# A hybrid retention, attention and expert layer on one core: the modulation products as four strips of 32 columns, a fifth row buffer, norm scaling on ScalarE, and a new order

## The chip, the core and the metric

The kernel runs on one core of one Trainium2 chip. A core has a matrix engine (TensorE, PE in the profile; its weight loads are listed apart as PEld), VectorE (DVE), ScalarE (ACT), GpSimd (POOL) and SyncE (SP), which work at the same time and wait for one another through semaphores. Operands lie in an on-chip memory of 128 partitions (SBUF); PE adds its results up in banks of a second one (PSUM). The transfers from and to the large memory (HBM) are done by 16 DMA engines; here SP issues most of them, and POOL those that gather rows by index. The metric is the device time of one execution in microseconds (us), the median of several runs.

## What is computed

One layer for 1024 latent tokens and 256 context tokens of width D = 1024, in fp32. Cut to what matters:

```python
mod   = silu(c)     @ w_mod + b_mod        # 6 x 1024 numbers: shift, scale, gate, twice
mod_c = silu(c_ctx) @ w_mod + b_mod        # for the context tokens: shift and scale are used
h  = rms_norm(x,   norm1_g) * (1 + mod[1])   + mod[0]
hc = rms_norm(ctx, norm1_g) * (1 + mod_c[1]) + mod_c[0]
rq, rk, rv, rg, dq, dk, dv = split(h @ w_in)       # the same for hc
y  = concat(retention_both_ways(...), differential_attention(...))
x  = x + mod[2] * (y @ w_out)
h2 = rms_norm(x, norm2_g) * (1 + mod[4]) + mod[3]
q  = h2 @ w_query                          # 8 heads, two halves of 128
experts, gate = top 16 of the sums of the top 16 by two sets of 128 keys
x  = x + mod[5] * sum_j gate_j * gelu(peer_u[experts_j] . h2) * peer_v[experts_j]
```

`w_mod` has 1024 x 6144 numbers (24 MB). There are 128 x 128 = 16384 experts, each a row of 1024 numbers in `peer_u` and in `peer_v`, and each token uses 8 x 16 = 128 of them.

## The kernel before

**How the order of the work comes about.** The kernel does not issue its instructions as it reads. A recording layer (class `Plan`, lines 162 to 590) keeps each operation as a node, with a cost in us by a table of rules (`cost`, line 281), and a list scheduler (`schedule`, line 332, run several times) places them on the five engines by rank. Ranks come from the order of recording; where several stages are to overlap, `weave` (line 207) merges their recordings, each stretched over a span of the others from a pair of constants (`QSPAN`, `ASPAN`, `GSPAN`, `G2SPAN`, `HSPAN` and others at the top of the file). Then all is issued in the planned order from one line (590; 591 in the changed kernel), so every instruction of the trace shows that line and groups are told apart by the names of their tiles. SBUF tiles come from pools by tag, each with a number of buffers (`bufs`, line 602); a tile waits until one of its tag is free.

**Stages.** The 10 blocks of 128 tokens are 8 latent ones (0 to 7) and 2 of the context.

1. *The start.* Five blocks are loaded and scaled by their norms (`norm_rows`, line 675: two squares with sums on ScalarE, the power -0.5 on GpSimd, the scaling on VectorE). The first 2048 columns of `w_mod` come in 8 chunks of 1024 x 256 (1 MB, two `wst` tiles each, which has 4 buffers, `wstream`, line 666). For each chunk, 8 products add up in one PSUM tile: the weights are `sc[:, k, :]`, 128 rows of which only 2 columns are used (silu of `c` and of `c_ctx`), the moving operand is 128 x 256 of `w_mod`. The two rows go to `mrow`, 16 transposes turn them to columns (`modT`), and `token_cols` (715) applies them.
2. *Projections.* `project3` (860) multiplies five key blocks by chunks of `w_in`, then the five others: each fp32 factor is split into two fp32r parts (ACT takes the high part, DVE the rest), and three products stand for one (`three`, 851). That split recurs in the dense phase.
3. *Retention* (1005), with the queries of block 0 (`late_queries`, 960) and `spread(0)` to `spread(2)` (1068) woven in. A spread does four more chunks of `w_mod` as above, for one of the four vectors `mod[2..5]`, adds the bias and stores the row in HBM; `spread(3)` is woven into the routing of block 0.
4. *By groups of blocks* (0; 4 and 5; 6 and 7; 3; 1 and 2): `attend`, `mix` (output projection), `route` (queries and key scores), `select` (1283: the top 16, by many small DVE steps), and, for blocks 3 to 7, `gates` (1417), which lays the gates out as a dense table `Wd` in HBM.
5. *The dense phase* (1500) for blocks 3 to 7: all 16384 experts by products, in 32 groups of 4 x 128 experts; each group loads 4 rows of `peer_u`, 4 of `peer_v` (all split) and its part of `Wd`.
6. *Gathered rows* for blocks 0, 1 and 2 (`halves`, 1368), beside stages 4 and 5: 2 x 3 x 128 = 768 times POOL gathers 128 rows of `peer_u` or `peer_v` by index into a tile of 128 x 1024 (512 KB), and DVE does one step on it: a product with a sum along the row (`gat,act<-gat,h2t`), or the sum `acc<-gat,act,acc`. The tiles are taken from the tag `gat` (4 buffers) or, when more than 5 of its 8 are free, from `h`. In a window of the plan (`HOLD`) POOL issues no gathers, so that the selection and the gates have DVE.

Of the kernel before, what the change touches and what calls it, by code (L numbers as in the profile page):

```python
# [31 lines left out]
HOLD = [1000, 1550]  # L32
# [20 lines left out]
QSPAN = [[-0.2, 0.475], [0.1, 1], [-0.1, 1.309], [-0.35, 1.05], [0.15, 0.9]]  # L53
ASPAN = [[0.05, 1.424], [0.05, 1.05], [0.15, 1], [0, 1.104]]
GSPAN = [[0.3, 1], [-0.15, 0.754], [0.15, 1.248], [-0.1, 1.2], [-0.3, 0.02]]
DSPAN = [0.02, 0.0, 0.05]
LSPAN = [[0.479, 1.05], [0.565, 1.218], [0.436, 1.3], [0.05, 0.85]]
G2SPAN = [0.182, 0.991]
VL, CL, EC, XE = 'D', 'D', 'D', 'PPPPPPPP'
POFF, PACES = 40, [[0, 3.6], [200, 2.25], [300, 1.17], [700, 1.18], [1100, 1.9]]  # L60
# [8 lines left out]
HSPAN = [[-0.25, 1.0], [0.05, 0.796], [0.2, 1.588]]  # L69
# [92 lines left out]
class Plan:  # L162
# [118 lines left out]
    def cost(self, eng, meth, a, k, outs, vs):  # L281
# [19 lines left out]
        if eng == "PE":  # L301
# [6 lines left out]
            return 4 * max(n, 64) * (0.5 if n >= 256 and a[1].shape[0] == 64 else 1) / 2330.0, 0, None, False  # L308
# [288 lines left out]
def layer(tc, I, out, dbg=None):  # L597
# [3 lines left out]
    with sp as S, pp as P, dp as DR:  # L601
        bufs = {"mm": 8, "h": 8, "k": 5, "rv": 4, "b": 4, "v": 5, "sel": 3, "wst": 4, "gat": 4, "fin": 2,  "u1": 3, "u2": 2, "u3": 2,
                "o": 1, "vi": 2, "egb": 3, "pt": 2, "m4": 4, "s1": 2, "act": 2,  "gsum": 2, "rs": 2, "ssum": 2, "ff": 3}
# [15 lines left out]
        def ps(shape):  # L619
            return nc.tile(shape, F32, "mm")  # L620
# [36 lines left out]
        cc = sb([128, KD, 2], "cc")  # L657
# [5 lines left out]
        sc = sb([128, KD, 2], "sc")  # L663
        nc.scalar.activation(sc, cc, AF.Silu)
# [10 lines left out]
        def norm_rows(kb, tag):  # L675
# [11 lines left out]
            nc.vector.tensor_scalar(xt, xt, ms[:, 2:3], None, op0=OP.mult)  # L687
# [5 lines left out]
        rcol = sb([128, 24], "rcol")  # L693
# [3 lines left out]
        mrow = [sb([2, D], "rv") for _ in range(2)]  # L697
        for ch in range(8):
            w = wstream(wm, ch * 256)
            pm = ps([2, 256])  # L700
            with nc.unit():
                for k in range(KD):
                    nc.tensor.matmul(pm, sc[:, k, :], w[k], start=(k == 0), stop=(k == KD - 1))
            nc.scalar.copy(mrow[ch // 4][:, ch % 4 * 256:(ch % 4 + 1) * 256], pm)
        mt = ps([128, 16, 2])
        with nc.unit():
            for n in range(16):
                nc.tensor.transpose(mt[:, n, :], mrow[n // 8][:, n % 8 * 128:(n % 8 + 1) * 128], ident[0:2, 0:2])
# [44 lines left out]
        dist = sb([128, 2, 128], "vi")  # L753
        nc.sync.dma_start(dist, I["k_dist"])
# [6 lines left out]
        retg = sb([128, 512], "pt")  # L761
        nc.sync.dma_start(retg, row_bcast(I["ret_norm_g"], 512))
# [869 lines left out]
```

## Time and profile before

| what | us |
|---|---|
| median of 3 runs (lowest to highest) | 3445.88 (3432.36 to 3452.61) |
| the profiled execution's own time | 3449.74 |
| its span in the trace | 3447.9 |
| ACT busy, of the span | 1330.9 (39%) |
| POOL busy, of the span | 1115.0 (32%) |
| the costliest group: `mm<-k,h` on PE, 4096 records (the dense phase's products with `peer_u`) | 925.5 |
| transfers | 809.69 MB, 235 GB/s in the mean |

The mean granted clock of TensorE was 0.960 of full speed. In rows of groups, `out<-in` are tile names (buffer numbers left out): `mm` is any PSUM tile, `wst` a buffer of streamed weights, `sc` the two condition vectors, `rv` and `h` are shared by many uses (in the start `rv` holds the two modulation rows, in the dense phase `h` holds split expert rows), `gat` the gathered rows, `egb` the expert indices. `x384 | 86.1, 379` are the count, the busy us and the mean ns of one; what follows is the idle time just before them and what ended it. An fp32 product shows as two records.

### The profile page before, as it was taken

Reading aid. Unit: us, or ns where it says so; the run is one execution under the profiler, and the core shown is the slowest. Engines: PE = TensorE matmul, PEld = TensorE weight load, DVE = VectorE, ACT = ScalarE, POOL = GpSimd, SP = SyncE. Lnnn points to the kernel's source line nnn. Section 1 sums busy time; section 2 is a strip of 40 time slices with the busy share of each in tenths; the row PEclk is TensorE's granted clock in tenths of the full one; section 3 lists DMA queues with packets and bytes.
Section 4 is the critical chain, followed back from the end, with each engine's and each line's share of the span. In section 5 each row is a group of like instructions: output and inputs, shape, how many; then the busy total and the mean of one; then the engine's idle time right before and its main releaser. Section 6 shows DMA issues by size and latency. Waiting matters only on the chain. (4 is left out here: it accounts for less than half of the span.)

```text
span 3447.9 us, 51507 instructions
## 1 busy us (share of the span) xinstructions
PE 3151.3 (91%) x18240; PEld 2732.3 (79%) x18240; DVE 2654.8 (77%) x5963; ACT 1330.9 (39%) x3535; POOL 1115.0 (32%) x1099
## 2 busy tenths in 40 slices
PE   7999997779789888897899999999999999999998
PEld 4998575557677766887788888989898889788887
DVE  4457546879997978666978888788888887878797
ACT  4342443425269898753212222222222222222221
POOL 0101111443440201103544444344444443444341
PEclk9999998889999998999999999999999999999999
DMA  5322655777584642654888889798888887878886
GB/s 184 97 82 88 214 194 169 262 272 238 182 292 155 217 138 93 219 194 159 287 296 275 308 273 307 244 305 282 298 287 310 278 307 271 283 258 296 284 289 207
DMA packets 314532, 809.69 MB, mean 235 GB/s; under 512 B 29313, under 2 KB 125593, under 8 KB 314274
## 3 DMA queue, kind: packets, MB, share of 16 engines
q1 hardware_dynamic: 203682, 403.70, 35.1%
q0 software_dynamic: 110592, 402.70, 34.3%
q8 instruction: 144, 2.36, 0.3%
q14 instruction: 114, 0.93, 0.1%
HBM read 745.46 MB, written 60.83 MB: 234 GB/s over the span
## 5 line engine op out<-in xcount | busy, mean ns | idle before, releaser
L590 PE MATMUL mm<-k,h 128*128 128x384 f32 (+1 forms) x4096 | 925.5, 311 | 34.4 <-DVE h L590 32.1
L590 PEld LDWEIGHTS mm<-k,h 128*128 128x128 f32 x4096 | 700.0, 189 | 46.9 <-DVE h L590 33.8
L590 POOL DMA_INDIRECT gat<-peer_v,egb x379 | 465.2, 1227 | 640.8 <-DVE acc L590 432.2
L590 ACT CAST h<-wst 128x512 fp32r<-128x512 f32 (+1 forms) x384 | 286.6, 762 | 895.4 <-PE mm L590 869.3
L590 PE MATMUL mm<-v,h 128*128 128x384 f32 (+1 forms) x2048 | 632.1, 309 | 0.0
L590 POOL DMA_INDIRECT gat<-peer_u,egb x369 | 439.0, 1190 | 589.4 <-DVE gat L590 386.1
L590 PE MATMUL mm<-h,rv 128*128 128x512 f32 x2304 | 602.1, 399 | 17.5 <-DVE rv L590 12.4
L590 DVE SCALAR_TENSOR_TENSOR acc<-gat,act,acc 128x1024 f32<-128x1024 f32 x376 | 483.2, 1285 | 64.1 <-DMA gat<-peer_v,egb 62.6
L590 PEld LDWEIGHTS mm<-h,rv 128*128 128x128 f32 x2304 | 425.1, 190 | 119.4 <-DVE rv L590 21.4
L590 DVE SCALAR_TENSOR_TENSOR gat<-gat,h2t 128x1024 f32<-128x1024 f32 x369 | 452.3, 1231 | 48.2 <-DMA gat<-peer_u,egb 47.8
L590 DVE TENSOR_TENSOR h<-wst,h 128x512 fp32r<-128x512 f32 (+1 forms) x384 | 329.3, 867 | 204.9 <-issue 109.4
L590 PE MATMUL mm<-h,t 128*128 128x512 f32 (+1 forms) x1600 | 419.8, 393 | 26.8 <-DVE b L590 16.9
L590 PEld LDWEIGHTS mm<-v,h 128*128 128x128 f32 x2048 | 387.5, 189 | 7.9
L590 PEld LDWEIGHTS mm<-h,t 128*128 128x128 f32 x1600 | 294.4, 189 | 100.3 <-DVE b L590 22.7
L590 POOL TENSOR_TENSOR m<-m,mhalf 128x4 f32<-128x4 f32 (+1 forms) x78 | 75.5, 970 | 771.2 <-DVE m L590 761.5
L590 PE MATMUL mm<-b,wst 128*128 128x256 f32 (+1 forms) x1280 | 237.3, 340 | 0.6 <-ACT h L590 0.3
L590 PEld LDWEIGHTS mm<-b,wst 128*128 128x128 f32 x1280 | 204.0, 192 | 24.3 <-ACT u L590 2.6
L590 ACT CAST rv<-aT 128x384 fp32r<-128x384 f32 x128 | 65.8, 514 | 355.8 <-DVE aT L590 349.8
L590 DVE TENSOR_TENSOR b<-b,mm 128x512 f32<-128x512 f32 x248 | 164.9, 682 | 43.8 <-PE mm L590 43.6
L590 PE MATMUL mm<-t,h 128*128 128x256 f32 x992 | 186.8, 287 | 6.7 <-DVE aT L590 3.5
L590 PEld LDWEIGHTS mm<-t,h 128*128 128x128 f32 x992 | 158.1, 193 | 8.0 <-DVE aT L590 3.7
L590 PE MATMUL mm<-wst,h 128*128 128x256 f32 x560 | 156.5, 297 | 0.0
(239 smaller groups left out, 4714.5 us busy)
## 6 DMA issues: line engine op xcount, KB each, us to landing
wst<-peer_u_cols SPq DMA_DIRECT2D x128, 512.0 KB, 7.1
wst<-peer_v_halves SPq DMA_DIRECT2D x128, 512.0 KB, 4.5
wst<-w_query_chunks SPq DMA_DIRECT2D x80, 512.0 KB, 5.3
h<-Wd SPq DMA_DIRECT2D x64, 512.0 KB, 9.7
wst<-w_mod_chunks SPq DMA_DIRECT2D x48, 512.0 KB, 5.2
wst<-w_out_chunks SPq DMA_DIRECT2D x40, 512.0 KB, 7.1
Wd<-rv SPq DMA_DIRECT2D x40, 512.0 KB, 6.8
Wd<-gat SPq DMA_DIRECT2D x40, 512.0 KB, 5.7
```

The source lines that it names most:

```text
L590: getattr(handles[n.eng], meth)(*[res(v) for v in a], **k)
```

## The change

It has four parts. The computation stays the same.

1. **Strips.** `sc` becomes 128 x 8 x 32 with zeros in all but two columns of each 32 (in the tag `ob`, set to zero by DVE). A new function `conditioned` does the 8 products of a chunk: product k goes to partitions 32 (k mod 4) and on of one PSUM tile, so that four sums of two products each lie in four strips of 32 partitions. All 128 partitions are copied. A selector `pick` (128 x 2, ones in rows 32 g and 32 g + 1, made from the identity) adds the four strips: in the start 16 products with 128 x 128 weights and `pick` as the moving operand take the place of the 16 transposes of 2 x 128; in a spread two products with one column of `pick` as weights and 512 moving columns are new, and the bias is added from PSUM in two steps of 1 x 512. The planner's cost of such a product is set to 0.3 of a full one.
2. **A fifth `gat` buffer** (2 MB to 2.5 MB for the tag). Small tiles move to tags that exist: `cc`, `rcol`, `t8`, `sc`, one of two tiles in `gates`, and the retention's mask and gain (`t4`, `t6`), which are now computed and loaded at the beginning of `retention` and not in the start.
3. **Norm scaling** in `norm_rows` moves from DVE to ACT (18 calls).
4. **Order.** `HOLD` ends at 1500 of the plan and not 1550; some pairs of the spans change. (`QSPAN[4]` is not used, and the last entry of `PACES` begins at step 1100 of 768.)

```diff
-HOLD = [1000, 1550]
+HOLD = [1000, 1500]
-HSPAN = [[-0.25, 1.0], [0.05, 0.796], [0.2, 1.588]]
+HSPAN = [[-0.4, 1.0], [0.05, 1.096], [0.2, 1.888]]
...
-            return 4 * max(n, 64) * (0.5 if n >= 256 and a[1].shape[0] == 64 else 1) / 2330.0, 0, None, False
+            side = 0.3 if outs[0].shape[0] == 32 else 0.5 if n >= 256 and a[1].shape[0] == 64 else 1
+            return 4 * max(n, 64) * side / 2330.0, 0, None, False
...
-        bufs = {"mm": 8, "h": 8, "k": 5, "rv": 4, "b": 4, "v": 5, "sel": 3, "wst": 4, "gat": 4, "fin": 2,  "u1": 3, "u2": 2, "u3": 2,
+        bufs = {"mm": 8, "h": 8, "k": 5, "rv": 4, "b": 4, "v": 5, "sel": 3, "wst": 4, "gat": 5, "fin": 2,  "u1": 3, "u2": 2, "u3": 2,
...
-        sc = sb([128, KD, 2], "sc")
-        nc.scalar.activation(sc, cc, AF.Silu)
+        sc = sb([128, KD, 32], "ob")
+        nc.vector.memset(sc, 0.0)
+        nc.scalar.activation(sc[:, :, 0:2], cc, AF.Silu)
+        pick = sb([128, 2], "pick")
+        nc.vector.tensor_reduce(out=pick, in_=ident.rearrange("p (g c) -> p c g", c=32)[:, 0:2, :], axis=AX.X, op=OP.add)
+        def conditioned(w):
+            pm = ps([128, 256])
+            with nc.unit():
+                for k in range(KD):
+                    g = k % 4 * 32
+                    nc.tensor.matmul(pm[g:g + 32, :], sc[:, k, :], w[k], start=(k < 4), stop=(k >= 4))
+            return pm
...
-            nc.vector.tensor_scalar(xt, xt, ms[:, 2:3], None, op0=OP.mult)
+            nc.scalar.activation(xt, xt, AF.Copy, scale=ms[:, 2:3])
...
-        mrow = [sb([2, D], "rv") for _ in range(2)]
+        mrow = [sb([128, D], "rv") for _ in range(2)]
         for ch in range(8):
             w = wstream(wm, ch * 256)
-            pm = ps([2, 256])
-            with nc.unit():
-                for k in range(KD):
-                    nc.tensor.matmul(pm, sc[:, k, :], w[k], start=(k == 0), stop=(k == KD - 1))
-            nc.scalar.copy(mrow[ch // 4][:, ch % 4 * 256:(ch % 4 + 1) * 256], pm)
+            nc.scalar.copy(mrow[ch // 4][:, ch % 4 * 256:(ch % 4 + 1) * 256], conditioned(w))
...
-                nc.tensor.transpose(mt[:, n, :], mrow[n // 8][:, n % 8 * 128:(n % 8 + 1) * 128], ident[0:2, 0:2])
+                nc.tensor.matmul(mt[:, n, :], mrow[n // 8][:, n % 8 * 128:(n % 8 + 1) * 128], pick, start=True, stop=True)
...
-                nc.scalar.copy(row[:, ch * 256:(ch + 1) * 256], pm)
-            nc.vector.tensor_tensor(out=row[0:1, :], in0=row[0:1, :], in1=bro, op=OP.add)
+                nc.scalar.copy(row[:, ch * 256:(ch + 1) * 256], conditioned(w))
+            for half in range(2):
+                hs = slice(half * 512, (half + 1) * 512)
+                pm = ps([1, 512])
+                nc.tensor.matmul(pm, pick[:, 0:1], row[:, hs], start=True, stop=True)
+                nc.vector.tensor_tensor(out=bro[:, hs], in0=bro[:, hs], in1=pm, op=OP.add)
...
-                    o1 = sb([128, 4, 128], "t4" if q % 2 else "o")
+                    o1 = sb([128, 4, 128], "t4" if q % 2 else "t7")
```

Three places show how the order moves. The first is PE's queue from the program's beginning in the kernel before (`mm<-wst,sc` are the chunk products, `mm<-ident,rv` the transposes of the two rows, `mm<-ident,k` those of token blocks):

```order
L590 MATMUL mm<-ident,k 128x128
L590 MATMUL mm<-ident,act 128x24
L590 MATMUL mm<-ident,k 128x128 x15
L590 MATMUL mm<-wst,sc 2x256 x64
L590 MATMUL mm<-ident,rv 128x2 x16
L590 MATMUL mm<-ident,k 128x128 x24
```

And in the changed kernel, where `sc` lies in a tile of the tag `ob`:

```order
L591 MATMUL mm<-ident,act 128x24
L591 MATMUL mm<-ident,k 128x128 x8
L591 MATMUL mm<-wst,ob 32x256 x16
L591 MATMUL mm<-ident,k 128x128 x8
L591 MATMUL mm<-wst,ob 32x256 x48
L591 MATMUL mm<-pick,rv 128x2 x16
L591 MATMUL mm<-ident,k 128x128 x24
```

The first two chunks now stand between the transposes of token blocks, and the products with `pick` where the transposes of the rows stood. The second place is DVE's queue in the second dense group, before (`h<-wst,h 128x1024` is a split of one row of `peer_u`; `sel` belongs to the selection of block 2). The split at the end of these rows is that of the row numbered 7; the last split ahead of it stands 67 instructions earlier, and 17 of the 66 between are steps on gathered rows:

```order
L590 TENSOR_TENSOR sel<-sel 128x800
L590 SCALAR_TENSOR_TENSOR acc<-gat,act,acc 128x1024
L590 TENSOR_REDUCE sel<-sel 128x4x4
L590 SCALAR_TENSOR_TENSOR gat,act<-gat,h2t 128x1024
L590 CAST egb<-sel 128x128
L590 TENSOR_TENSOR h<-wst,h 128x1024
```

In the changed kernel, at the splits of rows 5 and 6 (row 7's comes 4 instructions later); row 4's stands 40 instructions ahead of row 5's, with 2 steps on gathered rows among the 39 between:

```order
L591 TENSOR_TENSOR sel<-sel 128x640
L591 TENSOR_TENSOR h<-wst,h 128x1024
L591 SCALAR_TENSOR_TENSOR gat,act<-gat,h2t 128x1024
L591 SCALAR_TENSOR_TENSOR acc<-gat,act,acc 128x1024
L591 TENSOR_REDUCE sel<-sel 128x4x8
L591 SCALAR_TENSOR_TENSOR gat,act<-gat,h2t 128x1024
L591 TENSOR_TENSOR sel<-sel 128x640
L591 TENSOR_REDUCE sel<-sel 128x4x8
L591 TENSOR_TENSOR sel<-sel 128x560
L591 SCALAR_TENSOR_TENSOR gat,act<-gat,h2t 128x1024
L591 SCALAR_TENSOR_TENSOR acc<-gat,act,acc 128x1024
L591 TENSOR_TENSOR h<-wst,h 128x1024
```

Row 7's split now stands ahead of the selection's last steps and of most gathered rows; row 5's has moved behind a long part of the selection. The third place is POOL's queue at the pause, before (`DMA gat<-peer_u,egb` is a gather; the last row is a norm's power in the stretch without gathers):

```order
L590 DMA gat<-peer_u,egb 128x1024
L590 DMA h<-peer_u,egb 128x1024
L590 TENSOR_TENSOR t_7690<-t_7690,t_8920 128x512
L590 DMA gat<-peer_v,egb 128x1024 x2
L590 TENSOR_TENSOR m_10285<-m_10285,mhalf 128x4
```

And in the changed kernel:

```order
L591 TENSOR_TENSOR t_8010<-t_8010,t_8941 128x512
L591 DMA gat<-peer_u,egb 128x1024
L591 DMA h<-peer_u,egb 128x1024
L591 DMA gat<-peer_u,egb 128x1024
L591 DMA gat<-peer_v,egb 128x1024 x2
L591 DMA h<-peer_u,egb 128x1024
L591 DMA gat<-peer_u,egb 128x1024
L591 DMA h<-peer_v,egb 128x1024
L591 DMA h<-peer_u,egb 128x1024
L591 DMA gat<-peer_v,egb 128x1024
L591 DMA h<-peer_u,egb 128x1024 x2
L591 TENSOR_TENSOR m_10288<-m_10288,mhalf 128x4
```

Before, 115 gathers stand ahead of the pause, now 131; the last of all stands one dense group sooner than before. On DVE most of block 0's selection now stands behind the attention of block 4's last head, and on PE block 5's selection transposes stand behind two more projections.

## What I predict

> **What bounds the kernel now.** I read the page first, then the windows over the whole span, then the waits of PE, then the groups by form that the change touches. The page has PE busy in 91% of the span:
>
> ```profile
> PE 3151.3 (91%) x18240; PEld 2732.3 (79%) x18240; DVE 2654.8 (77%) x5963; ACT 1330.9 (39%) x3535; POOL 1115.0 (32%) x1099
> ```
>
> The windows show which stretch has which limit. The columns are the stretch, its length, then busy us (and instructions) of PE, PEld, DVE, ACT and POOL, the granted clock, the DMA share and GB/s.
>
> ```profile
> 100.00:200.00 100.00, 98.73 (x830) 97.81 (x828) 57.04 (x150) 45.06 (x118) 12.84 (x15) 1.00 0.29 94
> 300.00:400.00 100.00, 95.78 (x633) 64.74 (x632) 56.11 (x121) 28.67 (x55) 9.47 (x10) 0.98 0.57 181
> ...
> 500.00:600.00 100.00, 78.73 (x508) 61.74 (x507) 71.54 (x302) 39.76 (x113) 15.23 (x35) 0.85 0.54 173
> ...
> 900.00:1000.00 100.00, 76.62 (x367) 64.66 (x366) 92.41 (x219) 31.97 (x91) 59.18 (x62) 0.86 0.81 277
> 1000.00:1200.00 200.00, 181.57 (x1168) 159.16 (x1166) 178.52 (x647) 170.91 (x608) 27.94 (x59) 0.96 0.60 203
> ...
> 2000.00:2500.00 500.00, 487.38 (x2673) 434.28 (x2672) 407.33 (x641) 127.22 (x244) 214.72 (x178) 0.99 0.85 287
> 2500.00:3000.00 500.00, 493.37 (x2741) 442.31 (x2740) 414.16 (x648) 129.10 (x249) 221.22 (x181) 1.00 0.84 289
> ```
>
> Up to 400 us and in the dense phase (from about 1500 us) PE is busy for 96 to 99% of the time: there PE work taken away is time taken away, if nothing else is late. From 500 to 1000 us PE is busy for 77 to 79% only, and DVE for up to 92%. So PE's 297 us of idle time (3447.9 less 3151.3) lie mostly in the middle, and the waits name who ends them: us in total, number, longest.
>
> ```profile
> PE mm L590 <- DVE u L590: 54.9, 22, 15.9
> PE mm L590 <- DVE h L590: 45.7, 21, 23.9
> ...
> PE mm L590 <- DVE sel L590: 16.2, 4, 14.3
> ```
>
> Three of these are long: 15.9 us (attention of blocks 4 and 5 behind the selection of block 0 on DVE), 23.9 us (a split of a row of experts, in the second dense group, behind the selection of block 2 and gathered rows on DVE), and 14.3 us (transposes for the selection of block 5, in PE's queue ahead of work that was ready).
>
> **The strips, in PE time.** The groups by form, with busy us and mean ns:
>
> ```profile
> L590 PE MATMUL mm<-wst,sc 128*2 128x256 f32 x384 | 86.1, 379 | 2.3 <-DMA wst<-w_mod_chunks 1.8 <-ACT sc L590 0.4
> L590 PE MATMUL mm<-v,aT 128*128 128x128 f32 x512 | 75.5, 290 | 6.1 <-ACT aT L590 5.9
> L590 PEld LDWEIGHTS mm<-v,aT 128*128 128x128 f32 x512 | 67.2, 202 | 17.1 <-ACT aT L590 7.6 <-issue 7.1 <-ACT ff L590 0.8
> L590 PE MATMUL mm<-rv,u 128*64 128x128 f32 x120 | 10.3, 287 | 0.8 <-DVE u L590 0.8
> ```
>
> An fp32 product has two records, so 384 are the 24 chunks of 8 products, and a chunk costs 86.1 / 24 = 3.59 us. Nothing in before uses quarters of the array, but the retention's products of 64 columns go to its two halves: 10.3 / 60 = 0.172 us each, where the full-width ones of the same 128 moving columns cost 75.5 / 256 = 0.295 us. Two halves thus run at 0.58 of the serial price. Two such steps give 0.34, or 1.2 us for a chunk; the bounds are a perfect quarter, 0.9 us, and no overlap at all, 3.59 us. I take 1.2, since the halves are the nearest row: 24 x 2.39 = 57 us less on PE. The Trainium skill ("TensorE: Matmul & The Clock Gate", Part 3, Measured speedup vs the span model) has three column strips at 2.38 times the speed; if four did no better here, a chunk would cost an estimated 1.5 us and the sum below would be 4 us poorer in the spreads. No run here shows strips of 32.
>
> The selectors give some back. At the start 16 products with 128x128 weights and 2 moving columns stand in place of 16 transposes that took 1.17 us in all (row below). Their two weight loads each, by the load row above at 0.20 us, bound them at 6.4 us; taken: 4, so 3 more. In each spread two products of one weight column with 512 moving columns are new: by the chunk products (86.1 / 192 = 0.45 us for 256) 0.9 us each, 7 us in four spreads. PE work falls by 57 - 3 - 7 = 47 us in all.
>
> **Where that lies.** PE time in the chunk products alone, by stretch:
>
> ```profile
> 20.00:40.00 20.00, 18.45 (x86) 6.99 (x85) 0.00 (x0) 1.00 0.86 289
> 40.00:60.00 20.00, 8.87 (x40) 3.08 (x38) 0.00 (x0) 0.92 0.39 135
> 100.00:400.00 300.00, 36.06 (x162) 13.02 (x163) 0.00 (x0) 0.99 0.36 113
> ```
>
> *The start (8 chunks).* The timeline (start, us):
>
> ```profile
> 18.72 7.23 PE L590 MATMUL mm<-wst,sc 128*2 128x256 f32 x32 [0.39 <-ACT sc L590]
> ...
> 21.95 20.04 SPq L590 DMA_DIRECT2D wst<-w_mod_chunks  x12
> ...
> 41.92 7.35 PE L590 MATMUL mm<-wst,sc 128*2 128x256 f32 x32 [0.28 <-DMA wst<-w_mod_chunks]
> ...
> 49.20 1.17 PE L590 MATMUL mm<-ident,rv 2*128 2x2 f32 x16
> ```
>
> The products run from 18.72 to 49.27 us, and all later work needs their sums. Twelve of the sixteen half-chunk loads of 512 KB go out from 21.95 us on, each when PE frees a buffer; with PE faster they are bound by the transfers. At the 289 GB/s of 20 to 40 us those 6.3 MB take 21.8 us: the last product would end at about 21 + 21.8 + 1.2 = 44. If the loads gain nothing, only the last chunk's own 2.4 us go; if they ran at a third more than 289 GB/s, they would end 5 us sooner than 44. I take 41, 8 earlier, less 3 for the selectors: **-5** (-11 to +2).
>
> *Spreads 0 to 2 (12 chunks, 10 of them between 100 and 400 us).* PE is 96% busy in the window from 300, the DMA share is 0.57, and no wait of PE is long up to 440 us, so these 12 x 2.39 - 5.4 = 23 us are on the path. Two things eat at it: a chunk is 1 MB and now comes due sooner, and the retention's mask (4 + 4 small DVE steps and its constants' loads) is now computed in that stretch instead of under the start's loads, a few us of DVE at 56% busy. **-18** (-25 to -6). *Spread 3* (4 chunks, near 500 us) lies where PE waits for DVE: **-1** (-9 to 0).
>
> **The order.** The instructions that front.md shows change place; each is priced at its wait.
>
> *440 to 1000 us.*
>
> ```profile
> PE mm L590 <- DVE u L590: 40.8, 12, 15.9
> PE mm L590 <- DVE sel L590: 15.2, 2, 14.3
> ```
>
> The selection of block 0 now stands on DVE behind what PE waited 15.9 us for, and block 5's transposes stand later on PE. Both stalls go from their places; but DVE has the same work to do, and at 92% busy the next thing that PE wants is late instead. Of 30 us I take **-4** (-15 to +5).
>
> *16 more gathered rows ahead of the pause.* Each costs a DVE step:
>
> ```profile
> L590 DVE SCALAR_TENSOR_TENSOR acc<-gat,act,acc 128x1024 f32<-128x1024 f32 x376 | 483.2, 1285 | 64.1 <-DMA gat<-peer_v,egb 62.6
> L590 DVE SCALAR_TENSOR_TENSOR gat<-gat,h2t 128x1024 f32<-128x1024 f32 x369 | 452.3, 1231 | 48.2 <-DMA gat<-peer_u,egb 47.8
> ```
>
> 16 x 1.26 = 20 us of DVE in 900 to 1200 us, where DVE is 89 to 92% busy (29 us free of 300, in pieces). They cost nothing if they fall into the pieces, 20 if none does; PE has its own idle time there (42 us), so **+8** (0 to +20). That the gathers end one dense group sooner gains nothing, since the last groups are PE's.
>
> *The second dense group.* The 23.9 us wait was for one split that stood behind 66 instructions in DVE's queue, 17 of them steps for gathered rows and most others the selection's:
>
> ```profile
> PE mm L590 <- DVE h L590: 30.9, 4, 23.9
> ```
>
> Now at most 39 stand between two splits there, 2 of them for gathered rows. By their count the wait would be 24 x 39 / 66 = 14 us; by the gathered rows alone, 15 x 1.26 = 19 us shorter. **-10** (-20 to +5).
>
> **The fifth row buffer.** DVE waited 62.6 + 47.8 = 110 us for gathered rows (the two rows above). A buffer more lets POOL ask one row earlier, so part of that goes, but PE, not DVE, bounds the dense phase (487 and 493 of 500 us). PE's own waits there are small; **-4** (-14 to 0, beside the rival below on transfers). The small tiles that share a tag now wait for nothing that the trace shows late; nothing for that (0 to +3).
>
> **Scaling by norms on ScalarE.** 18 DVE steps of 0.75 us go, and 18 ACT steps come; a 128x1024 step of ACT is nearest by its cast:
>
> ```profile
> 11.05 0.75 DVE L590 TENSOR_SCALAR k<-k,m 128x1024 f32<-128x1024 f32 x1 [0.69 <-POOL m L590]
> ...
> L590 ACT CAST h<-wst 128x1024 fp32r<-128x1024 f32 x128 | 134.2, 1048 | 659.3 <-PE mm L590 654.6 <-DVE u L590 4.0 <-DMA wst<-peer_u_cols 0.7
> ```
>
> DVE -13.5, ACT +18.9 us. At the start five of them delay the squares of the next block and the copies of the sums by 0.3 us each beside transfers; the others help DVE where it is late. **-2** (-6 to +3).
>
> **Sum.** -5 - 18 - 1 - 4 + 8 - 10 - 4 - 2 = -36. The profiled run took 3449.7 us, so 3414 there; it is 3.9 above the median of the runs (3445.88), which I take off: **3410 us**, 1.0% less. A measurement of this kernel tells about 0.5%, 17 us, from no change; its runs differ by 20.
>
> **The rivals.**
>
> (a) *The strips do not overlap.* Then a chunk stays at 3.59 us, PE gains nothing, and the selectors cost 10 us: the start gives +3 in place of -5, the spreads +5 in place of -18, spread 3 +1 in place of -1, and the sum is -3: **3443**, no change. For it: no row has quarters, and in the spreads each chunk stands between full-width products. Against it: the halves at 0.58 lie between full-width products too. Chance 0.07. The Trainium skill ("TensorEngine Tiling (Array Packing)", Key Properties) says that changing the tiling mode drains TensorE, which would eat part of the gain at both ends of each chunk; the halves' row, measured with such changes, bears it out only as far as its 0.58.
>
> (b) *DVE takes it all back between 440 and 1700 us.* PE is ahead by 23 us at 440, but DVE's work is the limit until the dense phase: the gathers cost +20, the stalls +3, the second dense group -2, and the rest stands: -36 + 12 + 7 + 8 = -9, **3437**. For it: DVE at 92% from 900, and PE waits for DVE more than for anything else. Against it: the stalls of 30 us are gone from their places, and 29 us of DVE were free. Chance 0.13.
>
> (c) *The earlier end of the pause makes it slower.* Gathers resume 50 us sooner in the plan (the pause ends at 1500 instead of 1550). If the rows come while the selection of blocks 1 and 2 is on DVE, 50 / 1.26 = 40 rows bring 50 us of DVE work. Between 1550 and 1650 DVE was busy as follows:
>
> ```profile
> 1550.00:1600.00 50.00, 43.77 (x227) 39.41 (x226) 29.80 (x79) 17.78 (x34) 7.92 (x14) 0.93 0.41 132
> 1600.00:1650.00 50.00, 26.14 (x158) 24.42 (x157) 43.63 (x112) 8.50 (x16) 28.11 (x32) 0.80 0.67 208
> ```
>
> 27 us were free, so 23 us would lie on the path in place of the -10, and with the other gathers at +20 the sum is -36 + 33 + 12 = +9: **3455**, slower. With 10 us more on top it passes 0.5%. It decides if DVE is full from the pause's end to the selection's and PE's wait for DVE's splits grows past 24 us. For it: the wait is there already. Against it: the new order on DVE has fewer gathered rows between the splits than before. Chance 0.10.
>
> (d) *More is gained.* The fifth buffer and the moved stalls give their good ends: -15 and -20 in place of -4 and -10, -14 in place of -4: -36 - 31 = -67, **3379**. For it: 110 us of DVE's waits for rows. Against it: PE hardly waits in the dense phase. Chance 0.18.
>
> **How the numbers follow.** The forecast has the remaining 0.52, with its own range of 3395 to 3432 (two of its terms at half their bad or good ends). The range must leave out 2 in 10 at most: 3380 to 3443 leaves out (c) and about half of (d). Faster by over 0.5% (under 3428.7): 0.93 of the forecast, all of (d), a little of (a) and (b): 0.69. Slower by over 0.5% (over 3463): the worse part of (c) and mishaps of the forecast: 0.07. The rest, 0.24, is no change.
>
> **What would show it.** Strips: a chunk's 8 products within 1.2 us from first to last, 24 chunks at some 29 us of PE time; near 3.6 each would be (a). Start: the selector's products at about 41 to 44 us instead of 49.20. At 400 us the same work some 23 us earlier than before, the gain of start and spreads. The waits of PE for DVE between 440 and 1000 us lower by 4 to 15 us in total; if they grow by what PE gained, it is (b). The longest wait in the second dense group at 14 us; over 24, it is (c). DVE's waits for gathered rows clearly under 110 us; if dense groups are shorter as well, (d). Wrong altogether would be PE waits for weights (none to speak of now) in the dense phase, or a lower granted clock there.

## The result and the profile after

The changed kernel takes **3333.52 us** (median of 4 runs, 3332.61 to 3334.88), the kernel before beside it 3439.12 (4 runs, 3431.02 to 3452.61): a ratio of **0.969**, with a 95% interval of 0.9667 to 0.9712. It is 106 us faster, where 36 had been forecast, and lies below the range. The span of its profile is 3331.5 us, 116.4 less than before. The page of the changed kernel:

```profile
PE 3088.1 (93%) x18272; PEld 2710.2 (81%) x18272; DVE 2635.5 (79%) x5951; ACT 1341.7 (40%) x3553; POOL 1146.8 (34%) x1099
```

PE is busy for 63 us less, and its idle time has gone from 297 us to 243. The windows of the changed kernel say where (columns as before):

```profile
0.00:50.00 50.00, 26.40 (x177) 13.88 (x178) 10.54 (x71) 24.09 (x49) 6.72 (x26) 0.78 0.82 290
...
300.00:400.00 100.00, 83.91 (x686) 61.45 (x681) 63.14 (x140) 31.76 (x65) 10.02 (x10) 0.93 0.57 192
...
900.00:1000.00 100.00, 80.34 (x395) 66.58 (x395) 91.36 (x236) 46.43 (x131) 47.39 (x50) 0.88 0.84 281
1000.00:1200.00 200.00, 171.03 (x1055) 148.09 (x1054) 183.02 (x649) 163.41 (x590) 35.41 (x65) 0.94 0.60 202
...
1600.00:1700.00 100.00, 96.77 (x521) 84.92 (x520) 88.24 (x137) 27.28 (x49) 49.51 (x39) 1.00 0.88 308
...
2000.00:2500.00 500.00, 499.80 (x2779) 450.48 (x2778) 423.22 (x661) 131.97 (x252) 230.79 (x185) 1.00 0.86 297
2500.00:3000.00 500.00, 499.07 (x2772) 449.37 (x2771) 422.58 (x659) 131.82 (x251) 234.83 (x187) 1.00 0.86 298
```

In the dense phase PE is now busy for all of the time (499.8 and 499.1 of 500 us), and more products pass in a window. From 300 to 400 us it is busy for 84 us instead of 96: work went away there and idle time came in its place. The stages of the two profiled runs, and of three experiments told below, each by the end of its last product on PE (PE's records, counted off against the order of the program), in us:

| stage | before | changed | a_gat4 | a_plan4_real5 | a_serial_same |
|---|---|---|---|---|---|
| first projection begins | 58.1 | 58.0 | 59.8 | 58.4 | 63.5 |
| retention begins | 292.0 | 294.6 | 298.2 | 295.5 | 301.2 |
| attention of block 0 ends | 452.0 | 449.7 | 452.8 | 452.7 | 473.1 |
| output projection of blocks 4, 5 ends | 689.6 | 662.3 | 670.8 | 664.9 | 688.8 |
| last routing product | 1540.1 | 1514.2 | 1532.1 | 1513.1 | 1540.2 |
| second dense group ends | 1658.2 | 1607.3 | 1652.5 | 1634.5 | 1633.7 |
| third dense group ends | 1717.9 | 1666.6 | 1710.0 | 1690.5 | 1692.6 |
| last dense group ends | 3412.2 | 3294.4 | 3392.3 | 3315.5 | 3319.4 |
| one dense group, 3rd to 26th | 58.19 | 56.14 | 57.98 | 56.02 | 56.11 |

So of the 118 us that separate the ends of the last group, 2 arise up to 450 us (23 forecast, with the start), 24 up to the routing's end, 25 in the first two dense groups, and 67 in the thirty after them, 2.2 us in each.

*The start.* The timeline of PE (start, us) in the changed kernel:

```profile
18.98 3.64 PE L591 MATMUL mm<-wst,ob 128*32 128x256 f32 x32 [1.82 <-ACT ob L591]
...
25.19 0.64 PE L591 MATMUL mm<-wst,ob 128*32 128x256 f32 x8 [0.73 <-ACT k L591]
...
33.89 2.28 PE L591 MATMUL mm<-wst,ob 128*32 128x256 f32 x16 [0.68 <-DMA wst<-w_mod_chunks]
...
41.15 2.25 PE L591 MATMUL mm<-wst,ob 128*32 128x256 f32 x16 [1.63 <-DMA wst<-w_mod_chunks]
43.34 6.99 PE L591 MATMUL mm<-pick,rv 128*128 128x2 f32 x32
50.19 5.15 PE L591 MATMUL mm<-ident,k 128*128 128x128 f32 x24
```

The products end at 43.34, within the 41 to 44 that were forecast, and PE waits for each chunk's transfer. But the 16 selector products take 6.99 us and not 4, so the token blocks' transposes begin at 50.19, as before at 50.30. And a chunk takes 2.28 us there, where half a chunk took 0.64 us at 25.19. The mean clock of 0.78 in the first row above hides two parts: up to 27.7 us the granted clock was 1.00, and from then to 55 us it was 0.50, under the other chunks, the selectors and most of the transposes. The windows of the changed kernel for the chunks and the selectors, and below them the same stretch of the kernel before:

```profile
28.00:43.30 15.30, 10.70 (x80) 2.13 (x80) 4.92 (x21) 6.19 (x13) 0.00 (x0) 0.50 0.90 326
43.30:50.30 7.00, 7.00 (x37) 6.96 (x34) 0.00 (x0) 0.37 (x1) 0.00 (x0) 0.50 0.22 82
```
```profile
28.00:50.00 22.00, 21.00 (x105) 8.26 (x103) 4.75 (x17) 3.00 (x8) 0.00 (x0) 1.00 0.77 260
```

So the 6 us by which the products ended sooner were lost again in the selectors, which at half the clock took 5.8 us longer than the transposes that they replace, and the first projection begins as before (58.0 against 58.1).

*The groups that were forecast.*

```profile
L591 PE MATMUL mm<-wst,ob 128*32 128x256 f32 x384 | 36.0, 480 | 15.1 <-DMA wst<-w_mod_chunks 11.9 <-ACT ob L591 1.8 <-ACT k L591 0.7
...
L591 PE MATMUL mm<-h,pick 128*1 128x512 f32 x16 | 9.1, 651 | 0.0
L591 PE MATMUL mm<-pick,rv 128*128 128x2 f32 x32 | 7.0, 353 | 0.0
```

A chunk costs 36.0 / 24 = 1.5 us in the mean (1.2 forecast). The products fell by 50 us and the selectors cost 16.1 - 1.2 = 15: PE's net gain is 35 us, not 47.

*The gathered rows.*

```profile
L591 DVE SCALAR_TENSOR_TENSOR acc<-gat,act,acc 128x1024 f32<-128x1024 f32 x374 | 480.6, 1285 | 6.4 <-DMA gat<-peer_v,egb 5.0
L591 DVE SCALAR_TENSOR_TENSOR gat<-gat,h2t 128x1024 f32<-128x1024 f32 x368 | 450.5, 1229 | 17.5 <-DMA gat<-peer_u,egb 17.5
```

DVE now waits 22.5 us for them in all, where it waited 110. PE's waits for DVE, over the whole span:

```profile
PE mm L591 <- DVE u L591: 52.9, 24, 9.0
PE mm L591 <- ACT t L591: 42.3, 54, 3.7
PE mm L591 <- DVE t L591: 23.2, 12, 6.0
PE mm L591 <- DVE h L591: 14.3, 15, 4.7
...
PE mm L591 <- DMA wst<-w_mod_chunks: 11.9, 10, 2.8
```

The waits of 15.9, 23.9 and 14.3 us are gone; the longest for DVE is 9.0. Those for split rows (`h`) went from 45.7 to 14.3 us in total.

### The profile page after: what moved, and what is told of

Read it like the earlier page. It is cut to its first block, busy times and chain, and to the rows that moved or that the text cites. A ratio compares the mean times of both kernels' runs of the same rounds, so it can differ in the third digit from the quotient of the medians.

```text
span 3331.5 us, 51447 instructions
## 1 busy us (share of the span) xinstructions
PE 3088.1 (93%) x18272; PEld 2710.2 (81%) x18272; DVE 2635.5 (79%) x5951; ACT 1341.7 (40%) x3553; POOL 1146.8 (34%) x1099
## 4 chain that ended last, share of the span: by engine, by line
PE 54%; DVE 10%; ACT 6%; issue 3%; DMA 2%; POOL 1%; DVEq 0%; POOLq 0%; SPq 0%; ACTq 0%
PE mm L591 54%; ACT t L591 2%; DVE sel L591 2%; DVE acc L591 2%; ACT rv L591 1%; DVE gat L591 1%; DVE t L591 1%; ACT gat L591 1%; DVE h L591 1%; DMA gat<-peer_v,egb 1%; POOL gat L591 1%; DVE vi L591 1%; ACT h L591 1%; DVE m L591 1%; DMA gat<-peer_u,egb 1%
## 5 line engine op out<-in xcount | busy, mean ns | idle before, releaser
L591 POOL DMA_INDIRECT gat<-peer_u,egb x368 | 474.0, 1288 | 555.4 <-DVE acc L591 341.4
L591 PE MATMUL mm<-h,rv 128*128 128x512 f32 x2304 | 586.7, 395 | 2.6 <-DVE h L591 1.8
L591 PE MATMUL mm<-t,t 128*128 128x128 f32 x1280 | 193.6, 298 | 45.0 <-ACT t L591 38.5
L591 ACT ACTIVATE t<-ob,pt 128x128 f32<-128x128 bf16 x640 | 220.1, 419 | 21.5 <-DVE ob L591 10.7
L591 PEld LDWEIGHTS mm<-t,t 128*128 128x128 f32 x1280 | 173.4, 198 | 67.3 <-ACT t L591 58.4
```

What stands on the lines that cost most here:

```text
L591: getattr(handles[n.eng], meth)(*[res(v) for v in a], **k)
```

## The experiments

Two theories came out of the table. **B**: the fifth row buffer took the waits for rows out of DVE's queue, and so PE's waits for DVE. **O**: the new order did it. A third, **P**, is that every new plan lands elsewhere by luck. For the strips: **S**, their gain is lost up to 450 us; **T**, it is on the path. Differences from the kernel before are against its runs on the same chip.

**a_gat4**, the changed kernel with four row buffers:

```diff
-"gat": 5,
+"gat": 4,
```

> The changed kernel with 4 row buffers instead of 5, all else as it is. Theory B (the fifth buffer took DVE's waits for gathered rows away, and PE's waits for DVE in the dense phase with them): dense groups go back from 55.6 to about 57.5 us, DVE waits for gathered rows 60 to 100 us in all again, total 3385 to 3400. Rival O (the new order, with more gathers ahead of the pause and none in the last groups, made the dense phase faster): dense groups stay at 55.6 us, total 3333 to 3345. Rival P (any new plan lands elsewhere by luck): something between, with the loss spread over all stages.

Measured: 3433.21 us; ratio to before 0.9972 (0.9951 to 0.9993). Nearly the whole gain is gone, more than theory B had asked for: dense groups are at 57.98 us again, and the second dense group ends 45 us later than in the changed kernel. Both the plan and the run have one buffer less here.

**b_gat5**, the kernel before with the fifth buffer alone (and the small tiles, mask included, that pay for it):

```diff
-"gat": 4,
+"gat": 5,
...
-        mask = sb([128, H, 128], "pt")
+            mask = sb([128, H, 128], "t4")
```

> The kernel before with a fifth row buffer and the moved small tiles (the retention's mask and gain made inside retention), but with its own products, norm scaling and order constants. Theory B: dense groups of about 55.6 us, DVE waits for gathered rows under 20 us, 50 to 65 us less than before: 3375 to 3390. Rival O: dense groups stay at 57.5 us, 3430 to 3445. Rival P: between, spread over all stages.

Measured: 3404.24 us; 0.9883 (0.9862 to 0.9903). Dense groups take 56.37 us, as B has it; but the attention of block 0 ends at 474.6 us, 22.6 later than before, and 20 of that is still there at the routing's end. The buffer's gain in the dense phase is there. Why the stages ahead of it are late was not tried: the mask has moved, and the plan is a new one, under order constants that were chosen for four buffers.

**a_oldorder** and **a_nudge**, the changed kernel with all order constants of before, and with one of them moved a little:

```diff
-HOLD = [1000, 1500]
+HOLD = [1000, 1550]
...
-HSPAN = [[-0.4, 1.0], [0.05, 1.096], [0.2, 1.888]]
+HSPAN = [[-0.25, 1.0], [0.05, 0.796], [0.2, 1.588]]
```
```diff
-HSPAN = [[-0.4, 1.0], [0.05, 1.096], [0.2, 1.888]]
+HSPAN = [[-0.4, 1.0], [0.05, 1.096], [0.2, 1.8]]
```

> The changed kernel with all order constants of before (HOLD, QSPAN, ASPAN, GSPAN, G2SPAN, HSPAN). Theory B: dense groups stay at 55.6 us; what goes back is the 25 us between 440 and 1540 us and the 30 us in the first two dense groups or a part of it, total 3350 to 3390. Rival O: dense groups at 57.5 us as well, total 3410 to 3435. Rival P: any value in between, without one stage that explains it.

> The changed kernel with one constant of the order moved slightly (the end of the third pair of HSPAN from 1.888 to 1.8), which has no meaning of its own: how far another plan of the same work lands. Theory B and rival O: within 10 us of the changed kernel's 3333.5, dense groups 55.6 us. Rival P: more than 20 us away, and the stages differ from 500 us on.

Measured: 3385.92 (0.9831, 0.9811 to 0.9852) and 3365.53 us (0.9769, 0.9744 to 0.9794). In both the dense groups stay short (56.61 and 56.79 us), so theory O falls for the dense phase. But the nudge costs 32 us, spread over the stages: 13 by 450 us, 17 at the second dense group's end, the other 15 in the thirty groups after it. So theory P holds beside B: this plan made anew is some 30 us off the one that was chosen, and experiments that make the planner plan again can't price an edit to less than that. It also says that some 30 of the 106 us hang on the plan that was drawn: with the nudge's plan the same four parts gain 76.

**a_plan4_real5** takes the planner out: the order planned for four buffers, issued with five.

```diff
-nc = Plan(tc, pools, bufs, {"mm": RESERVE})
+nc = Plan(tc, pools, dict(bufs, gat=4), {"mm": RESERVE})
```

> The order of instructions planned for 4 row buffers, exactly that of a_gat4, issued with 5 real ones: the queues are the same, only a gather may start one row sooner. Theory B (what counts is how many rows are on their way on the chip): dense groups fall from 58.0 to 56.0 to 56.8 us, DVE waits for gathered rows there from 74 to under 25 us, total 3365 to 3390, about 55 us less than a_gat4. Rival B2 (the plan made for five buffers has a better order on DVE, and that is the gain): dense groups stay at 57.5 to 58.2 us, total 3415 to 3440.

Measured: 3355.22 us; 0.9731 (0.9696 to 0.9765). All queues are those of a_gat4, and 78 us are gone. The waits of DVE and PE in the dense phase, from 1720 to 3230 us, with four real buffers:

```profile
DVE acc L591 <- DMA gat<-peer_v,egb: 46.7, 36, 4.1
...
DVE gat L591 <- DMA gat<-peer_u,egb: 26.9, 26, 2.1
```
```profile
PE mm L591 <- DVE b L591: 11.4, 13, 2.4
PE mm L591 <- DVE rv L591: 9.3, 12, 1.9
PE mm L591 <- DVE t L591: 6.3, 5, 2.3
PE mm L591 <- ACT rv L591: 6.0, 4, 2.3
```

And with five, in the same order of instructions:

```profile
DVE acc L591 <- DMA gat<-peer_v,egb: 2.0, 4, 1.0
...
DVE gat L591 <- DMA gat<-peer_u,egb: 0.2, 1, 0.2
```
```profile
PE mm L591 <- DVE b L591: 0.2, 1, 0.2
```

The 74 us in which DVE waited for rows are gone, and with them the waits of PE for sums, splits and gates that stood behind in DVE's queue. The window of the dense phase with four buffers, and with five:

```profile
1720.00:3230.00 1510.00, 1475.25 (x8122) 1317.49 (x8120) 1242.61 (x1927) 383.43 (x735) 676.57 (x546) 1.00 0.85 288
```
```profile
1720.00:3230.00 1510.00, 1509.69 (x8408) 1362.47 (x8407) 1282.62 (x1979) 398.80 (x761) 711.33 (x568) 1.00 0.87 299
```

PE's idle time falls from 34.8 us to 0.3, and a record takes 0.1796 us in place of 0.1816, 1.1% less: about two thirds and one third of the 52 us by which more work passes in this window. Part of the longer records is the clock: with four buffers there were four spells of 3.4 us at half the clock in this window, with five none. The first of them:

```profile
2065.00:2069.00 4.00, 4.00 (x12) 3.12 (x11) 3.72 (x8) 1.56 (x2) 1.91 (x2) 0.57 0.97 343
```

Half of the four spells is 7 us, and by estimate that is the most that the clock can have of the 17 us. From the second dense group to the last it is 1739.8 - 1681.0 = 59 us; the other 19 arise before the routing's end, where rows are gathered too. This shows B with nothing else changed.

**a_gat4_lend**, four buffers and a loan from a tag that seemed free (`LENDERS` lists the tags whose tiles a gathered row may take, each with how many must stay free):

```diff
-LENDERS = [('gat', 0), ('h', 5)]
+LENDERS = [('gat', 0), ('k', 4), ('h', 5)]
```

> The changed kernel with 4 row buffers, but a gathered row may also take one of the 5 tiles of the tag k when all 5 are free, which is so only after the last attention (about 1350 us): a fifth row buffer for the dense phase alone. Theory B (what counts in the dense phase is how many rows can be on their way): dense groups 56.1 to 56.8 us, DVE waits for gathered rows there under 25 us, total 3365 to 3390. Rival (the fifth buffer works through what else uses the tag, or through the plan up to 1600 us): dense groups stay at 58.0 us, total 3420 to 3440.

Measured: 3434.25 us; 0.9971 (0.9952 to 0.9989). It decides nothing: its trace has no gather into a tile of `k`, whose tiles hold the dense phase's split tokens. It counts as a second plan with four buffers, 57.80 us a group.

**a_hold1550**, the pause of the gathers ending where it did before:

```diff
-HOLD = [1000, 1500]
+HOLD = [1000, 1550]
```

> The changed kernel with the gathers' pause ending at 1550 of the plan again. If the pause's end is what took the 25 us out of the first two dense groups, they take 82 us again between their ends and the total is 3350 to 3370. If the order on DVE did it by other means, that stays at 56 us and the total is within 10 us of 3333.5, or wherever a new plan lands, 3340 to 3365, with the loss elsewhere.

Measured: 3358.4 us; 0.9739 (0.9704 to 0.9773). At the second dense group's end it is within 1 us of the changed kernel (1607.8), and then the third takes 77 us instead of 59. PE's waits from 1550 to 1720 us:

```profile
PE mm L591 <- DVE b L591: 18.1, 2, 17.1
PE mm L591 <- DVE h L591: 2.9, 2, 2.5
```

The stall behind the selection of block 2, 23.9 us in the kernel before, is back as one wait of 17.1, a group later; a_oldorder has one of 15.0 there. So HOLD's end is worth 18 us at this place in this plan. Another 6 us arise from there to the last group. But the early end does not do it alone: from the last routing product to the end of the third dense group it is 152 us in the changed kernel, a_nudge and a_early, 166 in a_dvenorm, and 177 to 181 in a_gat4, a_plan4_real5, a_nostrips and a_gat4_lend, all with the pause ending at 1500; in the kernel before it is 178.

**a_dvenorm**, the scaling of the norms back on DVE:

```diff
-nc.scalar.activation(xt, xt, AF.Copy, scale=ms[:, 2:3])
+nc.vector.tensor_scalar(xt, xt, ms[:, 2:3], None, op0=OP.mult)
```

> The changed kernel with the norm scaling back on DVE. Theory N (kernels with the scaling on ScalarE gained 13 to 25 us between 450 and 690 us, those with it on DVE 3 to 4, because DVE is late there): from the end of attention of block 0 to the output projection of blocks 4 and 5 it takes 225 to 238 us instead of 212.6; dense groups stay at 56.1 us; total 3345 to 3375. Rival (the gain there comes from the order constants): that stretch stays within 5 us of 212.6.

Measured: 3365.13 us; 0.9761 (0.9727 to 0.9796). The stretch from block 0's attention to the output projection of blocks 4 and 5 takes 225.3 us instead of 212.6, the edge of what theory N asked for; at the second dense group's end it is 21 us late. PE's longest waits between 450 and 690 us in a_dvenorm:

```profile
PE mm L591 <- DVE wst L591: 13.6, 1, 13.6
PE mm L591 <- DVE u L591: 9.4, 4, 3.4
PE mm L591 <- DVE h L591: 5.9, 5, 2.1
PE mm L591 <- DVE ssum L591: 5.8, 1, 5.8
```

And in the changed kernel, where ACT scales the blocks:

```profile
PE mm L591 <- ACT wst L591: 11.2, 2, 9.7
```

Two blocks are scaled there (`wst`). In a_dvenorm POOL has the first one's norm at 557.2 us and DVE scales it at 569.2, behind the selection in its queue. In the changed kernel ACT scales that block at 557.9; but the second one's norm needs a small DVE step, which stands behind the same selection, and PE waits 9.7 us for that block. So the waits for scaled blocks differ by 2.4 us only, and the second block is done at 571.2 us instead of 578.7. In the twelve profiles with a plan of their own, this stretch takes 212 to 225 us with the scaling on ACT (eight of them) and 225 to 238 with it on DVE (before, b_gat5, b_strips, a_dvenorm). The two sets do not overlap, but a_dvenorm lies within 1 us of the other set, and each of the two spreads over 13 us. So up to 13 us may be the scaling's; that is not shown, and the whole 32 us are no more than the nudge cost.

**a_nostrips** and **b_strips**, the strips taken out of the changed kernel, and put alone into the kernel before:

```diff
-nc.tensor.matmul(pm[g:g + 32, :], sc[:, k, :], w[k], start=(k < 4), stop=(k >= 4))
+nc.tensor.matmul(pm, sc[:, k, :], w[k], start=(k == 0), stop=(k == KD - 1))
```

> The changed kernel with the chunk products, the transposes and the spreads of before; fifth buffer, norm scaling and order constants stay. Theory S (the strips' 57 us of PE time buy nothing up to 450 us, since the start is bound by transfers and selectors and the retention stretch by DVE and transfers): attention of block 0 ends at most 8 us later than the 449.7 us of the changed kernel, total 3335 to 3370. Rival T (strips are worth what they save on PE in the retention stretch): 20 us or more later at that point, total 3360 to 3400.

> The kernel before with the strips, the selectors and the planner's 0.3 for them; 4 row buffers, the old norm scaling, the mask in the start and the old order constants. Theory S: attention of block 0 ends within 8 us of the 452.0 us of before, total 3420 to 3445. Rival T: it ends 16 to 24 us earlier and the total is 3405 to 3425.

Measured: 3404.2 (0.99, 0.9884 to 0.9917) and 3448.63 us (1.002, 1.0007 to 1.0034). They contradict each other: alone the strips gain nothing, and attention of block 0 ends 2.7 us later than before; taken out they cost 71 us, and that attention ends 30 later. Of those 30, 12.5 arise ahead of the retention (307.1 against 294.6), where in the new plan PE waits 8.3 us for the late norms of blocks 3 and 6. Both are new plans, so neither prices the strips.

**a_serial_same** does, with the queues as they are:

```diff
-nc.tensor.matmul(pm[g:g + 32, :], sc[:, k, :], w[k], start=(k < 4), stop=(k >= 4))
+nc.tensor.matmul(pm[0:32, :], sc[:, k, :], w[k], start=(k == 0), stop=(k == KD - 1))
```

> The changed kernel with the same instructions in the same queues, but all 8 products of a chunk go to the first strip of 32 columns, one after the other, and copies and selectors read that strip alone: the strips' overlap is gone and nothing is planned anew. Chunks should cost about 3.6 us again, 50 us more of PE in all. Theory S (the start is bound by transfers, the retention stretch by transfers and DVE, and the strips' gain is lost there): attention of block 0 ends 5 to 12 us later than the 449.7 us of the changed kernel, and the total is 3338 to 3346. Rival T (what the strips save on PE is on the path, as a_nostrips's loss of 30 us by then and 71 in all would have it): it ends 20 to 30 us later and the total is 3353 to 3375.

Measured: 3357.3 us; 0.9761 (0.9735 to 0.9786). Its groups:

```profile
L591 PE MATMUL mm<-wst,ob 128*32 128x256 f32 x384 | 88.6, 387 | 2.5 <-ACT ob L591 1.8 <-ACT rv L591 0.4 <-DMA wst<-w_mod_chunks 0.3
...
L591 PE MATMUL mm<-pick,rv 32*128 32x2 f32 x32 | 4.1, 258 | 0.0
```

The overlap saves 88.6 - 36.0 = 52.6 us of PE and **23.8 us** of time: 6.6 in the start (301.2 against 294.6 where the retention begins), 16.8 in the retention stretch, and it is kept to the end (25.0 at the last group). Copies and selectors read the first strip alone here. The selectors take 4 us less of PE than in the changed kernel, nearly all of it where that one had the lower clock (4.1 against 7.0 us in the start), so the price contains what the overlap lost by the clock. Theory S falls, T holds. That the changed kernel stands only 2.3 us better than before at 450 us is not the overlap's doing: it earns 23, and the rest of the change, the strips' own selectors among it, costs 21 there.

**a_early** and **a_early2** move the start's selectors beside the transfers, the second without a new plan (12 of 16 products, moved in the finished order):

```diff
+        mt = ps([128, 16, 2])
         for ch in range(8):
...
-        mt = ps([128, 16, 2])
-        with nc.unit():
-            for n in range(16):
+            for n in (2 * ch, 2 * ch + 1):
```

> The changed kernel with the start's 16 selector products in pairs, each pair right after its chunk's copy, instead of all 16 after the last chunk. They took 6.99 us there, when PE had nothing else; 14 of them now lie beside the transfers. If they were what ate the start's gain, the first projection begins 5 to 6 us earlier than 58.0 us. By theory S most of that stays up to 290 us, where PE is busy. The total is 3327, plus or minus 30 for the new plan; if the rows of the first projection are late instead, it begins at 57 to 58 us as before.

> The changed kernel in its own planned order, with one thing moved: 12 of the 16 selector products of the start go out in pairs two chunks after their own, beside the transfers; 4 stay behind the last chunk. Nothing else changes its place, so no new plan blurs it. If the selectors on the path ate the start's gain, the first projection begins 4 to 5 us earlier than 58.0 us, and the total falls to 3327 to 3331, as PE is busy up to 290 us; if the stretch from 300 to 450 us (transfers, DVE) takes it back, the total stays at 3332 to 3335.

Measured: 3364.69 (0.9785, 0.9769 to 0.9801) and 3333.01 us (0.9663, 0.9636 to 0.9689). a_early is a new plan, 31 us off like the nudge, and its first projection begins at 58.3. In a_early2's timeline, the last selectors, and the first product of the projection:

```profile
44.82 2.72 PE L601 MATMUL mm<-pick,rv 128*128 128x2 f32 x12
47.41 4.95 PE L601 MATMUL mm<-ident,k 128*128 128x128 f32 x24
55.39 0.58 PE L601 MATMUL mm<-t,h 128*128 128x256 f32 x1 [3.04 <-DVE aT L601]
```

The projection begins 2.6 us sooner (55.39), not 4 to 5; 3 us are still there at the output projection of blocks 1 and 2, 1 at the second dense group, and at the last group it is 2 behind: no difference by the medians. It beats the changed kernel by nothing that can be measured.

## Why the prediction was wrong

The direction was right, the size was not: 106 us in place of 36. By the steps of the sum:

- **The fifth row buffer: -4 (-14 to 0) is the step that failed.** It measured -78 us with the queues held (a_gat4 to a_plan4_real5), 59 of them in the dense phase. The text said that PE's own waits there were small, and gave DVE's 110 us of waits for rows no way to PE. The rows quoted held a good part of it: 12.6 and 6.6 us of idle PE in the two windows of 500 us, or some 30 over the phase, and products that are longer in the first of them (487.38 / 2673 = 0.1823 us a record, 0.1798 after). PE was held up by DVE's queue for 2 us a group, a little at a time. Rival (d) named the mechanism with the good end at -15, so it came out at 3379 only.
- **The strips: right in mechanism, mis-sized.** A chunk took 1.5 us in the mean and not 1.2. Up to 450 us the overlap alone was forecast at 8 us in the start and 12 x 2.39 = 29 in the spreads, and earned 23. The start's products ended when forecast, but its -5 came out at 0: the 16 selectors took 6.99 us at a granted clock of 0.50, where 4 was taken and 6.4 the bound, and the prediction had no term for the clock. All selectors were 15 us and not 10.
- **The rest up to 450 us: forecast at about +14** (8 for selectors, 5 for the mask and the chunks' transfers), **measured +21** (from the 23 that the overlap saves and the 2.3 that the stages differ). The selectors can be 12.6 of it (5.8 in the start, 6.8 in three spreads); the mask in the retention and the transfers of the chunks (6.2 us of PE's waits between 300 and 450 us in the changed kernel) can be the others. How they share it was not tried: the mask's old place has no room beside the fifth buffer.
- **Norm scaling on ScalarE: -2 (-6 to +3), not measured by itself.** With the scaling back on DVE the stretch from 450 to 690 us is 13 us longer, in a plan made anew, and the waits for the scaled blocks (13.6 us on DVE, 11.2 on ACT) tell 2.4 of them. DVE's time was priced (13.5 us) and its place in the queue was not: one block lay 12 us behind the selection.
- **The order: -4 + 8 - 10.** The 14.3 and 15.9 us waits went, and the stretch from 450 us to the routing's end gained 24 us, of which 19 are the buffer's, if the held queues of a_gat4 tell it. Whether the 16 earlier gathers sent a bill can't be read off: what is left is 5 us, with the norms' unknown share in it. The two dense groups gained 25 us; 18 of that kind hang on HOLD's end in this plan (a_hold1550), and other plans with the same end do not have them. It was forecast as -10, by counting rows; the wait that was to be 14 us is under 5. Rival (c), that the earlier end would slow the kernel, did not come about in any plan tried.
- **The rivals (a) and (b)** are out: the strips overlap, and DVE took nothing back in the middle.
- **Two readings were too neat.** Before, PE was busy for 77 to 85% in the windows from 500 to 1000 us, not 77 to 79, and for only 73% from 1600 to 1700 us, inside what was called a dense phase at 96 to 99%. No term of the sum rests on either.

What stays open: the parts don't add up to 106 one by one (78 for the buffer, 24 for the strips, up to 13 for the norms, 18 for HOLD, less 21), because most of them were measured from different plans, and a plan made anew moves the time by some 30 us. Those 30 us are luck as far as the forecast goes: no step of it had a term for the draw of a plan, and the nudge's 3365.53 us would have lain below its range too.

## What to carry to other kernels

A wait of an engine that is not the bottleneck counts when the bottleneck's operands stand behind it in the same queue: of 74 us that DVE waited for rows, 52 were lost on PE, 2 in each group, though it was 98% busy. Before a buffer count is priced at nothing, add up the bottleneck's small idle times over the whole phase and the lengthening of its own instructions. Where a planner sets the order, hold the order and change one thing at run time (real buffers, the operands of a product); a new plan of the same work was worth 31 and 32 us here (a_early and a_nudge), more than most edits.

## What the runs showed of the hardware

- Four strips of 32 columns of fp32 with 256 moving columns take 15.95 / 12 = 1.33 us for 8 products in the spreads, against 3.6 one after the other. PE busy with the chunk products from 300 to 450 us in the changed kernel:

```profile
300.00:450.00 150.00, 15.95 (x192) 5.24 (x192) 0.00 (x0) 0.00 (x0) 0.93 0.52 173
```

  In the start, paced by transfers (a chunk every 3 us), the same 8 took 2.25 to 2.30 us at a granted clock of 0.50. It had fallen at 27.7 us, after a stretch in which PE was busy for 1.44 of 3.40 us (first row), and it stayed there through the 7.00 us in which the selectors kept PE busy. In a_serial_same, whose products kept PE busy, it was 1.00 (the other two rows):

```profile
24.30:27.70 3.40, 1.44 (x18) 0.34 (x16) 0.00 (x0) 3.40 (x5) 1.83 (x9) 1.00 1.01 366
```
```profile
28.00:51.60 23.60, 22.88 (x108) 11.37 (x106) 4.92 (x21) 11.43 (x21) 0.00 (x0) 1.00 0.76 252
0.00:50.00 50.00, 32.16 (x138) 16.45 (x139) 10.01 (x70) 23.78 (x48) 6.70 (x26) 1.00 0.81 269
```

  So part of what the strips save in the start is paid back as clock. The Trainium skill ("TensorE: Matmul & The Clock Gate", Part 1: The HAM clock gate) has the clock fall when PE idles; the rows agree, though PE was not wholly idle in the stretch before the fall.
- A product with 128 x 128 fp32 weights and 2 moving columns took as long as its weight loads: 6.99 us for 16, in which the weight loads were busy for 6.96 of 7.00 us, at a granted clock of 0.50. In a_serial_same 16 with 32 rows of weights took 4.10 us at a clock that was 1.00 for the first 3.2 us; rows and clock changed together, so what the rows are worth is not shown.
- Products took longer in the phase with gaps: 0.1816 us a record with four row buffers and 0.1796 with five, in the same order. The rows show a granted clock of 1.00 for both, rounded; with four buffers it fell to 0.50 four times, for 3.4 us each (0.57 in the window from 2065 to 2069 us), with five not once.
